# Moving the split of the last row from 640 + 384 to 576 + 448 columns in a row-sum kernel

## The chip, the cores and the metric

The kernel runs on one core of one Trainium2 chip. The metric is the device time of one execution in microseconds (us), the median over several runs. "Span" is the shorter time that the profile covers, from the first to the last instruction of the core. Before the change the first three runs took 162.91 us in the median (162.87 to 163.31).

## The reference

```python
def setup_inputs():
    batch, seq, dim = 32, 512, 1024
    return {"x": np.random.randn(batch, seq, dim).astype(np.float32), "multiplier": 0.5}

def reference(x, multiplier):
    return (np.sum(x, axis=-1) * multiplier).astype(np.float32)
```

There are 16,384 rows of 1024 numbers. Each of the 128 partitions sums 128 of them. 67 MB are read and 64 KB are written.

## The kernel before

The rows of a partition are taken in eight blocks of 16. In seven of them one load brings the whole block; DVE (VectorE) sums rows 0 to 7 and ACT (ScalarE) rows 8 to 15. The last block is loaded in five pieces, so that little is left to do after the last byte. Its last row comes in two parts, and DVE reduces each on its own.

```python
    def dve_span(t, r, lo, hi, dst, start=0.0):
        mid = (lo + hi) // 2
        nc.vector.tensor_tensor_reduce(          # adds the two halves elementwise,
            out=t[:, r, lo:mid],                 # sums the result, begins from `start`
            in0=t[:, r, lo:mid],
            in1=t[:, r, mid:hi],
            scale=mul,
            scalar=start,
            op0=ADD,
            op1=ADD,
            accum_out=dst,
        )

    # ... seven blocks ...

    c0 = (n_blocks - 1) * B
    t = x_pool.tile([P, B, D], fp32, name="xb")
    cut = 640
    pieces = [(0, 8), (8, 13), (13, 15)]
    for lo, hi in pieces:
        loads.append(nc.sync.dma_start(out=t[:, lo:hi, :], in_=x_rows[:, c0 + lo : c0 + hi, :]))
    for lo, hi in ((0, cut), (cut, D)):
        loads.append(nc.sync.dma_start(out=t[:, B - 1, lo:hi], in_=x_rows[:, c0 + B - 1, lo:hi]))
    # ... the store of the first seven blocks ...
    on_act = {4, 5, 6, 7, 11, 12, 14}
    for r in range(B - 1):
        if r in on_act:
            act_row(t, r, c0 + r)
        else:
            dve_span(t, r, 0, D, res[:, c0 + r : c0 + r + 1])
    dve_span(t, B - 1, 0, cut, part)                                      # reduction 1
    dve_span(t, B - 1, cut, D, res[:, rows - 1 : rows], start=part)       # reduction 2
    # ... the store of the last block ...
```

A reduction over N columns is N/2 elementwise sums. It appears in the profile as `CUSTOM_DVE_ANT_0`, followed by a short `DVE_READ_ACCUMULATOR2_ANT` that writes the total. Reduction 2 begins from `part`, the result of reduction 1, so it waits for two things: the landing of part 2, and `part`.

Of the kernel before, what the change touches and what calls it, by code (L numbers as in the profile page):

```python
# [1 line left out]

# [4 lines left out]


@with_exitstack
def kernel(  # L10
    ctx: ExitStack,
    tc: tile.TileContext,
    x: bass.AP,
    multiplier: float,
    out: bass.AP,
):







    nc = tc.nc
    P = nc.NUM_PARTITIONS
    fp32 = mybir.dt.float32
    ADD = mybir.AluOpType.add

    x_flat = x.flatten_outer_dims()
    N, D = x_flat.shape  # L30
    rows = N // P
    x_rows = x_flat.rearrange("(p c) d -> p c d", p=P)
    out_view = out.rearrange("b s -> (b s)").rearrange("(p c) -> p c", p=P)
    mul = float(multiplier)

    B = 16
    n_blocks = rows // B
    assert N == P * rows and rows == n_blocks * B

    x_pool = ctx.enter_context(tc.tile_pool(name="x", bufs=3))  # L40
    res_pool = ctx.enter_context(tc.tile_pool(name="res", bufs=1))
    sums = res_pool.tile([P, rows], fp32, name="sums")
    res = res_pool.tile([P, rows], fp32, name="res")
    part = res_pool.tile([P, 1], fp32, name="part")

    loads = []
    acts = []

    def act_row(t, r, col):
        acts.append(nc.scalar.activation(  # L50
            out=t[:, r, :],
            in_=t[:, r, :],
            func=mybir.ActivationFunctionType.Copy,
            scale=mul,
            accum_out=res[:, col : col + 1],
        ))

    def dve_span(t, r, lo, hi, dst, start=0.0):
        mid = (lo + hi) // 2
        nc.vector.tensor_tensor_reduce(  # L60
            out=t[:, r, lo:mid],
# [9 lines that stand above are left out]
    for b in range(n_blocks - 1):  # L71
        c0 = b * B
        t = x_pool.tile([P, B, D], fp32, name="xb")
        loads.append(nc.sync.dma_start(out=t, in_=x_rows[:, c0 : c0 + B, :]))  # L74
        h = B // 2
        nc.vector.reduce_sum(  # L76
            out=sums[:, c0 : c0 + h], in_=t[:, 0:h, :], axis=mybir.AxisListType.X
        )
        nc.vector.tensor_single_scalar(  # L79
            out=res[:, c0 : c0 + h],  # L80
            in_=sums[:, c0 : c0 + h],
            scalar=mul,
            op=mybir.AluOpType.mult,
        )
        for r in range(h, B):
            act_row(t, r, c0 + r)

    c0 = (n_blocks - 1) * B
    t = x_pool.tile([P, B, D], fp32, name="xb")
    cut = 640  # L90
    pieces = [(0, 8), (8, 13), (13, 15)]
    for lo, hi in pieces:
        loads.append(
            nc.sync.dma_start(  # L94
                out=t[:, lo:hi, :], in_=x_rows[:, c0 + lo : c0 + hi, :]
            )
        )
    for lo, hi in ((0, cut), (cut, D)):
        loads.append(
            nc.sync.dma_start(  # L100
                out=t[:, B - 1, lo:hi], in_=x_rows[:, c0 + B - 1, lo:hi]
            )
        )
    c1 = c0
    nc.sync.dma_start(out=out_view[:, 0:c1], in_=res[:, 0:c1])
# [6 lines that stand above are left out]
    dve_span(t, B - 1, 0, cut, part)  # L112
    dve_span(t, B - 1, cut, D, res[:, rows - 1 : rows], start=part)



    seen = nc.sync.nop()
    for i in loads[-8:] + acts[-1:]:
        tc.add_manual_dep(
            seen.ins,  # L120
            i.ins.name,
            mybir.DependencyInfo(mybir.DependencyClass.Sync, mybir.DependencyReason.DATA),
            reason="ends seen early",
        )
    store = nc.sync.dma_start(out=out_view[:, c1:], in_=res[:, c1:])
    tc.add_manual_dep(
        store.ins,
        seen.ins.name,
        mybir.DependencyInfo(mybir.DependencyClass.NoSync, mybir.DependencyReason.SCHED_ONLY),
        reason="in this order",  # L130
    )

    def start_loads_at_entry(nc_):



        entry, *rest = nc_.main_func.blocks
        is_sp = lambda i: i.engine == mybir.EngineType.SP
        is_load = lambda i: type(i).__name__ == "InstDMACopy"
        for block in rest:  # L140
            body = list(block.instructions)
            own = [i for i in body if is_sp(i)]
            if not any(is_load(i) for i in own):
                continue
            lead = []
            for i in own:
                if not is_load(i) or i.sync_info.on_wait:
                    break
                lead.append(i)
            names = {i.name for i in lead}  # L150
            block.instructions = [i for i in body if i.name not in names]
            head = list(entry.instructions)
            at = next(
                k for k, i in enumerate(head) if is_sp(i) and type(i).__name__ == "InstDrain"
            )
            entry.instructions = head[:at] + lead + head[at:]
            return

    nc.at_finalize(start_loads_at_entry)


# [1 line left out]
_INS = ['x', 'multiplier']  # L163
_OUTS = [((32, 512), 'float32')]

_NUMBERS = {'multiplier': 0.5}


# [26 lines left out]
```

## Time and profile before

| | before |
|---|---|
| median of the first three runs | 162.91 us |
| span of the profiled execution | 160.9 us |
| moved, mean rate | 67.18 MB, 418 GB/s |
| DVE busy, ACT busy | 42%, 42% |
| DMA's share of the chain that ended last | 86% |
| last landing of x to the issue of the last store | 0.715 us |

These lines are from the page of the kernel before: the span, the busy time of the engines, the DMA total, the chain that ended last by engine, and the issues of the last two loads (size, and us from issue to landing).

```profile
span 160.9 us, 236 instructions
...
DVE 68.1 (42%) x34; ACT 67.8 (42%) x127; POOL 0.2 (0%) x4
...
DMA packets 2017, 67.18 MB, mean 418 GB/s; under 512 B 480, under 2 KB 608, under 8 KB 736
...
DMA 86%; DVE 11%; SPq 1%; issue 0%; DVEq 0%
...
xb<-in_x_dram SPq DMA_DIRECT2D x1, 320.0 KB, 47.7
xb<-in_x_dram SPq DMA_DIRECT2D x1, 192.0 KB, 47.6
```

The kernel is bound by its loads. Everything up to the last piece happens while data streams in; only what follows the last bytes can be shortened by the cut. The timeline of the kernel before shows that tail (start in us, duration in us, engine, line, operation, and in brackets the idle time before it with what ended it):

```profile
156.64 0.69 DVE L60 CUSTOM_DVE_ANT_0 xb<-xb 128x512 f32<-128x512 f32 x1 [0.57 <-DMA xb<-in_x_dram]
157.26 0.08 DVE L60 DVE_READ_ACCUMULATOR2_ANT res<- 128x1 f32 x1
157.46 0.49 DVE L60 CUSTOM_DVE_ANT_0 xb<-xb 128x320 f32<-128x320 f32 x1
157.61 0.19 ACT L50 ACTIVATION_READ_ACCUMULATOR xb<-xb 128x1 f32 x1
157.87 0.08 DVE L60 DVE_READ_ACCUMULATOR2_ANT part<- 128x1 f32 x1
158.04 0.42 DVE L60 CUSTOM_DVE_ANT_0 xb<-xb,part 128x192 f32<-128x192 f32 x1
158.38 0.08 DVE L60 DVE_READ_ACCUMULATOR2_ANT res<- 128x1 f32 x1
158.62 0.34 SPq L125 DMA_DIRECT2D out_dram<-res  x1
```

Row 13 is done at 157.34. Reduction 1 is the 128x320 line at 157.46, reduction 2 the 128x192 line at 158.04, and the last store is issued at 158.62. The end of the chain of waits of the same execution (start, duration, what) reads:

```profile
109.78 47.66 DMA xb<-in_x_dram
157.43 0.02 issue
157.46 0.49 DVE xb L60
157.95 0.02 DVE part L60
157.97 0.07 issue
158.04 0.42 DVE xb L60
```

By this chain, part 1's load, then reduction 1, then `part` release reduction 2. "issue" is time in which the engine waited for nothing that the profile shows.

The chain does not show part 2's load. The landing records of the trace do. Each load has 16, one for each DMA engine, and the wait ends with the last of them. To the nanosecond, in us:

```
157.432  last engine of part 1 has landed
157.455  reduction 1 begins
157.873  accumulator read begins; 157.956 it ends, `part` is ready
157.908  last engine of part 2 has landed
157.936  DVE's own wait instruction for part 2 is released (ends 157.957)
158.042  reduction 2 begins
158.623  last store is issued
```

The Trainium skill, "DMA: Bandwidth & Descriptors", section "Why a DMA increments its semaphore by 16 and not by 1", says that each participating engine counts for itself and that only the full 16 mean that all data has landed. The trace agrees: the 16 landings of part 2 spread from 157.143 to 157.908. The separate wait instruction is what "Perfetto Trace Analysis", section "Identifying Dependency Chains", describes: an instruction that waits for several engines may have wait instructions inserted in front of it.

### The profile page before, as it was taken

Reading aid. Unit: us, or ns where it says so; the run is one execution under the profiler, and the core shown is the slowest. Engines: PE = TensorE matmul, PEld = TensorE weight load, DVE = VectorE, ACT = ScalarE, POOL = GpSimd, SP = SyncE. Lnnn points to the kernel's source line nnn. Section 1 sums busy time; section 2 is a strip of 40 time slices with the busy share of each in tenths; the row PEclk is TensorE's granted clock in tenths of the full one; section 3 lists DMA queues with packets and bytes.
Section 4 is the critical chain, followed back from the end, with each engine's and each line's share of the span. In section 5 each row is a group of like instructions: output and inputs, shape, how many; then the busy total and the mean of one; then the engine's idle time right before and its main releaser. Section 6 shows DMA issues by size and latency. Waiting matters only on the chain.

```text
span 160.9 us, 236 instructions
## 1 busy us (share of the span) xinstructions
DVE 68.1 (42%) x34; ACT 67.8 (42%) x127; POOL 0.2 (0%) x4
## 2 busy tenths in 40 slices
DVE  0000049700695008930099102990049700597453
ACT  3000049600694008920099001980039700596952
POOL 0000000000000000000000000000000000000000
DMA  7997997998998998998998998998998998999991
GB/s 261 522 440 342 522 440 342 522 424 359 522 424 359 522 424 359 522 424 359 522 424 361 522 407 375 522 407 375 522 407 375 522 407 375 407 448 396 425 386 40
DMA packets 2017, 67.18 MB, mean 418 GB/s; under 512 B 480, under 2 KB 608, under 8 KB 736
## 3 DMA queue, kind: packets, MB, share of 16 engines
q1 hardware_dynamic: 2016, 67.18, 97.2%
q14 instruction: 1, 0.01, 0.0%
HBM read 67.11 MB, written 0.07 MB: 418 GB/s over the span
## 4 chain that ended last, share of the span: by engine, by line
DMA 86%; DVE 11%; SPq 1%; issue 0%; DVEq 0%
DMA xb<-in_x_dram 86%; DVE sums L76 11%; SPq L94 1%; DVE xb L60 1%; SPq L74 0%; DVE part L60 0%; DVEq L190 0%
## 5 line engine op out<-in xcount | busy, mean ns | idle before, releaser
L50 ACT ACTIVATE xb<-xb 128x1024 f32<-128x1024 f32 x63 | 65.6, 1043 | 88.2 <-DMA xb<-in_x_dram 88.2
L76 DVE TENSOR_REDUCE sums<-xb 128x8 f32<-128x8192 f32 x7 | 60.8, 8686 | 85.0 <-DMA xb<-in_x_dram 85.0
L50 ACT ACTIVATION_READ_ACCUMULATOR xb<-xb 128x1 f32 x63 | 11.8, 187 | 0.0
L60 DVE CUSTOM_DVE_ANT_0 xb<-xb 128x512 f32<-128x512 f32 (+1 forms) x9 | 5.6, 667 | 5.1 <-DMA xb<-in_x_dram 4.9
L50 ACT ACT_TABLE_LOAD x1 | 1.3, 1283 | 1.7 <-PEq L176 1.7
L79 DVE TENSOR_SCALAR res<-sums 128x8 f32<-128x8 f32 x7 | 1.2, 172 | 0.2
L60 DVE DVE_READ_ACCUMULATOR2_ANT res<- 128x1 f32 x9 | 0.7, 83 | 0.0
L60 DVE CUSTOM_DVE_ANT_0 xb<-xb,part 128x192 f32<-128x192 f32 x1 | 0.4, 419 | 0.1
L176 POOL MEMSET const-uint8-127<- 128x1 uint8 x1 | 0.1, 103 | 0.0
L176 POOL MEMSET const-bfloat16-1.0<- 128x1 bf16 x1 | 0.1, 102 | 0.0
L176 POOL MEMSET const-float32-0.0<- 128x1 f32 x1 | 0.1, 99 | 0.2 <-issue 0.2
L176 POOL MEMSET const-float32-1.0<- 128x1 f32 x1 | 0.1, 99 | 0.0
L60 DVE DVE_READ_ACCUMULATOR2_ANT part<- 128x1 f32 x1 | 0.1, 83 | 0.0
## 6 DMA issues: line engine op xcount, KB each, us to landing
xb<-in_x_dram SPq DMA_DIRECT2D x1, 4096.0 KB, 39.6
xb<-in_x_dram SPq DMA_DIRECT2D x1, 2560.0 KB, 45.4
xb<-in_x_dram SPq DMA_DIRECT2D x1, 1024.0 KB, 47.4
xb<-in_x_dram SPq DMA_DIRECT2D x1, 320.0 KB, 47.7
xb<-in_x_dram SPq DMA_DIRECT2D x1, 192.0 KB, 47.6
xb<-in_x_dram SPq DMA_DIRECT2D x7, 49.3
out_dram<-res SPq DMA_DIRECT2D x1, 56.0 KB, 10.8
out_dram<-res SPq DMA_DIRECT2D x1, 8.0 KB, 1.4
```

The lines of the kernel that those rows point to most:

```text
L50: acts.append(nc.scalar.activation(out=t[:, r, :], in_=t[:, r, :], func=mybir.ActivationFunctionType.Copy, scale=mul, accum_out=res[:, col ...
L60: nc.vector.tensor_tensor_reduce(out=t[:, r, lo:mid], in0=t[:, r, lo:mid], in1=t[:, r, mid:hi], scale=mul, scalar=start, op0=ADD, op1=ADD, ...
L76: nc.vector.reduce_sum(out=sums[:, c0 : c0 + h], in_=t[:, 0:h, :], axis=mybir.AxisListType.X)
L79: nc.vector.tensor_single_scalar(out=res[:, c0 : c0 + h], in_=sums[:, c0 : c0 + h], scalar=mul, op=mybir.AluOpType.mult,)
L94: nc.sync.dma_start(out=t[:, lo:hi, :], in_=x_rows[:, c0 + lo : c0 + hi, :])
L176: nc = _bacc.Bacc("TRN2", target_bir_lowering=False, num_devices=1)
```

## The change

The cut between the two parts moves 64 columns to the left. Part 1 gets smaller, so it should land and be reduced sooner, while reduction 2 grows by 32 sums.

```diff
-    cut = 640
+    cut = 576
```

## The prediction

> **What bounds the kernel now.** DMA. The page gives 67.18 MB at a mean 418 GB/s over a span of 160.9 us; DVE and ACT are each busy 42%. The chain of waits is 86% DMA `xb<-in_x_dram`; it ends with the landing of the last row's first part, two DVE reductions of that row and the last store. Only this tail can change: bytes and instruction count stay.
>
> **The tail before** (timeline and landing records of the trace, us from the span's start):
> - Part 1 (640 columns): all sixteen engines landed at 157.432. DVE was free at 157.34 and waited for it; reduction 1 (320 sums, 493 ns) began at 157.455.
> - Its accumulator read, which makes `part`, ran 157.873 to 157.956.
> - Part 2 (384 columns) landed at 157.908. DVE waits for it in an instruction of its own, released at 157.936, 28 ns after the landing, ended at 157.957.
> - Reduction 2 (192 sums, starts from `part`, 419 ns) began at 158.042. Its accumulator read ended at 158.468, the store was issued at 158.623 and landed at 160.04.
>
> So reduction 2 had two releasers that tie within a nanosecond: `part` (157.956) and the wait for part 2 (157.957). The landing of this block's rows 0 to 7 shows the same form of wait binding: landed 148.035, released 148.063, again 28 ns.
>
> **What the change does.**
> 1. Part 1 shrinks from 2560 to 2304 B a partition. Packets took 103 ns (2560 B) and 66 ns (1536 B): 37 ns per 1024 B, so 94 and 75 ns after. Each engine moves eight of each: part 1 lands 8 x 9.4 = 75 ns sooner, at about 157.36. The sum per engine is unchanged, so part 2 still lands at about 157.91.
> 2. Reduction 1: 288 sums. The Trainium skill, "VectorE: DVE Perf Modes", section "The TRN2 errata", gives (N+151)/0.96 ns for an fp32 tensor_tensor. The trace agrees: 691 ns for 512 (687 to 693 measured), 491 for 320 (493). So 33 ns less; begin 157.38, `part` ready at about 157.85, 0.11 us sooner than now.
> 3. Reduction 2: 224 sums, 33 ns more, about 452 ns.
>
> **What lies on the critical path.** The 0.11 us that `part` gains is not collected: reduction 2 is then held by part 2's landing alone, which stays. It begins where it did (158.04 to 158.05) and takes 33 ns longer. The end and the store move 0.03 to 0.04 us later. The tie says 640 was already the balance point; 576 gives DVE more work after the last byte. Had part 2's landing not bound, the gain would have been 0.11 - 0.03 = 0.08 us, so even the rival is 0.05%.
>
> Predicted: 162.95 us (162.91 + 0.03 to 0.04), range 162.60 to 163.40. The range comes from the runs of before (162.87 to 163.31), far wider than the effect. Chances: faster by over 2% 0.01, within 2% 0.98, slower by over 2% 0.01.
>
> **What in the profile would show each step.**
> - The gap between the landings of parts 1 and 2 grows from 0.476 to about 0.55 us.
> - Reduction 1 about 460 ns, reduction 2 about 452 ns.
> - Reduction 2 begins about 0.135 us after part 2's landing (as now), but 0.19 us after `part` was ready (now 0.086).
> - The chain that ended last passes through part 2's DMA, not part 1 and reduction 1.
> - Last landing of x to the store's issue: 0.715 us before, about 0.75 after.
>
> **What would make it wrong.** Part 2 lands sooner because its packets or its completion cost less than the straight line says; then up to 0.08 us is gained. Or 1792 and 2304 B rows move worse than 1536 and 2560 B; then tenths are lost. Ordinary run-to-run noise would hide all of it.

## The result, and the profile after

| | before | after |
|---|---|---|
| median of 6 runs | 163.01 us | 163.11 us |
| lowest to highest | 162.87 to 163.31 | 162.90 to 163.16 |
| ratio, 95% interval | | 1.0003, 0.999 to 1.0016 |
| span of the profiled execution | 160.9 us | 161.3 us |

A ratio here is the mean time of one kernel's fast runs over that of the other's fast runs of the same rounds, so it is not quite the ratio of the medians in the table. The time is the same within 2%, and indeed within 0.2%.

The lines of the page of the kernel after that answer to those of before:

```profile
span 161.3 us, 236 instructions
...
DVE 68.1 (42%) x34; ACT 67.9 (42%) x127; POOL 0.2 (0%) x4
...
DMA packets 2017, 67.18 MB, mean 417 GB/s; under 512 B 480, under 2 KB 608, under 8 KB 736
...
DMA 86%; DVE 11%; SPq 1%; issue 0%; DVEq 0%
...
xb<-in_x_dram SPq DMA_DIRECT2D x1, 288.0 KB, 47.6
xb<-in_x_dram SPq DMA_DIRECT2D x1, 224.0 KB, 47.6
```

The bound is the same, and so are the bytes and the number of instructions. The timeline of the kernel after, same columns as before:

```profile
157.07 0.69 DVE L60 CUSTOM_DVE_ANT_0 xb<-xb 128x512 f32<-128x512 f32 x1 [0.57 <-DMA xb<-in_x_dram]
157.69 0.08 DVE L60 DVE_READ_ACCUMULATOR2_ANT res<- 128x1 f32 x1
157.79 0.46 DVE L60 CUSTOM_DVE_ANT_0 xb<-xb 128x288 f32<-128x288 f32 x1
158.03 0.19 ACT L50 ACTIVATION_READ_ACCUMULATOR xb<-xb 128x1 f32 x1
158.18 0.08 DVE L60 DVE_READ_ACCUMULATOR2_ANT part<- 128x1 f32 x1
158.46 0.45 DVE L60 CUSTOM_DVE_ANT_0 xb<-xb,part 128x224 f32<-128x224 f32 x1 [0.20 <-DMA xb<-in_x_dram]
158.83 0.08 DVE L60 DVE_READ_ACCUMULATOR2_ANT res<- 128x1 f32 x1
159.07 0.34 SPq L125 DMA_DIRECT2D out_dram<-res  x1
```

Two things are new. Reduction 1 is shorter (0.46) and reduction 2 longer (0.45). And DVE now stands idle 0.20 us in front of reduction 2, waiting for the DMA; the line of before had no such bracket. The end of the chain of waits of the kernel after:

```profile
110.70 47.62 DMA xb<-in_x_dram
158.32 0.03 issue
158.35 0.02 DVEq L60
158.37 0.09 issue
158.46 0.45 DVE xb L60
```

The chain now goes from part 2's load straight to DVE's wait instruction (`DVEq`) and reduction 2. `part` has left it.

The whole tail lies about 0.42 us later in this profile than in the one of before. That is not the cut: the load of rows 13 and 14, which comes ahead of anything the change touches, already landed 0.43 us later (157.049 against 156.621). Counted from that landing, part 1 landed after 0.720 us, against 0.811 before, and part 2 after 1.275 us, against 1.287 before. The experiments below show how much the arrival of the stream scatters.

### The profile page after: what moved, and what is told of

Read it like the earlier page. It is cut to its first block, busy times and chain, and to the rows that moved or that the text cites. A ratio compares the mean times of both kernels' runs of the same rounds, so it can differ in the third digit from the quotient of the medians.

```text
span 161.3 us, 236 instructions
## 1 busy us (share of the span) xinstructions
DVE 68.1 (42%) x34; ACT 67.9 (42%) x127; POOL 0.2 (0%) x4
## 4 chain that ended last, share of the span: by engine, by line
DMA 86%; DVE 11%; SPq 1%; issue 0%; DVEq 0%
DMA xb<-in_x_dram 86%; DVE sums L76 11%; SPq L94 1%; SPq L100 0%; DVE xb L60 0%; SPq L74 0%; DVEq L60 0%; DVEq L190 0%
## 5 line engine op out<-in xcount | busy, mean ns | idle before, releaser
L60 DVE CUSTOM_DVE_ANT_0 xb<-xb,part 128x224 f32<-128x224 f32 x1 | 0.5, 452 | 0.2 <-DMA xb<-in_x_dram 0.2
```

The lines of the kernel that those rows point to most:

```text
L60: nc.vector.tensor_tensor_reduce(out=t[:, r, lo:mid], in0=t[:, r, lo:mid], in1=t[:, r, mid:hi], scale=mul, scalar=start, op0=ADD, op1=ADD, ...
```

## The experiments

The theory is the prediction's: after the change reduction 2 is held by the landing of part 2, which doesn't move, and the only lasting effect is the 33 ns that reduction 2 grew by. Rival 1: the new row sizes (2304 and 1792 bytes) slow the loads, and this is where the first profile's extra 0.45 us of span come from. Rival 2: `part` still holds reduction 2, so that an earlier part 1 is worth something. Rival 3, for cuts to the right of 640: the landing of part 2 alone sets the end.

The measure is the *tail*, from the last landing of part 2 to the issue of the last store. It is the sum of three terms: landing to the beginning of reduction 2, the duration of reduction 2, and a rest of 0.160 to 0.164 us in every run. All are read from the records of each profile. All profiles had a granted clock of 1.0. Each row is one profile. The terms repeat well from profile to profile: where the landing holds reduction 2 behind the usual wait instruction, it begins after 132 to 135 ns; reduction 2 of one size and form differs by 2 ns at most; and the rest differs by 4 ns. The effect of 34 ns is well above that.

The tail starts at part 2's landing, so it cannot show whether that landing itself moved. Counted from the landing of rows 13 and 14, part 2 landed after 1.263 to 1.289 us in the five profiles with loads of 576 and 448 columns, and after 1.274 to 1.290 us in the three with 640 and 384. So no shift shows, but one as small as the effect would be lost in this scatter.

| run | gap, landing of part 1 to part 2 | `part` ready, after part 2's landing | reduction 2 begins, after part 2's landing | reduction 2 takes | tail |
|---|---|---|---|---|---|
| before (640) | 0.476 us | +0.048 us | 0.134 us | 419 ns | 0.715 us |
| after (576) | 0.555 | -0.064 | 0.134 | 452 | 0.749 |
| after_again (576) | 0.549 | -0.058 | 0.133 | 451 | 0.748 |
| compute_only | 0.471 | +0.019 | 0.134 | 452 | 0.748 |
| load_only | 0.537 | -0.046 | 0.133 | 417 | 0.712 |
| cut128 | 1.066 | -0.383 | 0.134 | 684 | 0.979 |
| cut668b | 0.441 | +0.098 | 0.135 | 404 | 0.700 |
| cut768 | 0.323 | +0.267 | 0.302 | 352 | 0.817 |
| cut896 | 0.165 | +0.490 | 0.526 | 285 | 0.974 |
| cut768_nopart | 0.293 | not waited for | 0.214 | 284 | 0.661 |
| part_in_row (640) | 0.468 | +0.055 | 0.132 | 361 | 0.655 |
| in_row668 | 0.480 | +0.057 | 0.133 | 347 | 0.640 |
| part_first576b | 0.559 | -0.068 | 0.164 | 451 | 0.777 |
| part_first_in_row576b | 0.529 | -0.037 | 0.163 | 395 | 0.721 |

### The changed kernel again

No edit; five timed rounds.

> The changed kernel once more, timed in five rounds. Theory (reduction 2 is held by the landing of part 2; only its own 33 ns are added): last landing of x to the store's issue 0.75 us again (0.749 in the first profile of after, 0.715 before), ratio 1.0002, which no timing here can tell from 1. Rival 1 (the 0.45 us by which the first profile of after is longer comes from the new row sizes, which slow the stream): ratio about 1.0025 and the first block again landing some 0.36 us later than in before. I expect the theory; the stream's arrival should scatter by tenths of a microsecond in both kernels.

Measured: tail 0.748 us. 162.94 us against 162.88 for before, ratio 1.0003 (0.9991 to 1.0016). The load of rows 13 and 14 landed at 156.768 us here, against 157.049 us in the first profile of the same kernel. In all profiles it landed between 156.62 and 157.15, although the code up to there is the same. So the extra span of the first profile is scatter of the stream, and rival 1 has no support: its ratio of 1.0025 lies outside the interval.

### The same move, eight times as far

```diff
-    cut = 640
+    cut = 128
```

> The same move, eight times as far: cut 128, part 2 of 896 columns (448 sums). Theory: reduction 2 begins 0.134 us after part 2's landing as before, takes 419 + 256 x 1.04 = 686 ns, so last landing to the store's issue is 0.715 + 0.267 = 0.98 us, and the time grows by 0.27 us, ratio about 1.0016. The gap between the landings of parts 1 and 2 is 896 x 1.235 ns = 1.11 us. Rival 2 (`part` still holds reduction 2): `part` is ready more than half a microsecond before the landing, so reduction 2 would begin before or at the landing and the tail would not grow by the whole 0.27 us. Rival 1: the stream itself lands later by more than the scatter.

Measured: `part` is ready 0.383 us before part 2 lands, and reduction 2 begins 0.134 us after the landing, just as before. It takes 684 ns. Tail 0.979 us, 0.264 more than before. 163.09 us against 162.88, ratio 1.0017 (1.0003 to 1.0031). This is the one place where a timing sees the effect, and at the expected size. Rival 2 falls for cuts to the left of 640.

The gap came out at 1.07 us instead of 1.11, a small miss.

### The compute half alone

Loads of 640 and 384 columns, reductions of 576 and 448.

```diff
-    dve_span(t, B - 1, 0, cut, part)
-    dve_span(t, B - 1, cut, D, res[:, rows - 1 : rows], start=part)
+    dve_span(t, B - 1, 0, 576, part)
+    dve_span(t, B - 1, 576, D, res[:, rows - 1 : rows], start=part)
```

> The compute half of the change alone: loads stay 640 and 384 columns, the reductions are 576 and 448 columns. Theory: the gap between the landings stays 0.476 us, reduction 2 (452 ns) begins 0.134 us after part 2's landing, last landing to the store's issue 0.749 us: all of the loss with no change of a transfer. Rival 1 (the row sizes of the loads matter): 0.715 us as before.

Measured: gap 0.471 us, reduction 2 begins after 0.134 us and takes 452 ns, tail 0.748 us. All of the loss is there without any change of a transfer.

### The load half alone

Loads of 576 and 448 columns, but reduction 2 leaves 64 columns out (a wrong result, relative error 0.02).

```diff
-    cut = 640
+    cut = 576
@@
-    dve_span(t, B - 1, cut, D, res[:, rows - 1 : rows], start=part)
+    dve_span(t, B - 1, 640, D, res[:, rows - 1 : rows], start=part)
```

> The load half of the change alone, WRONG RESULT ON PURPOSE in the last column of the output: loads are 576 and 448 columns, reduction 1 takes 576 columns, reduction 2 only the last 384 (64 columns are left out). Theory: gap between landings 0.55 us, `part` ready 0.2 us before reduction 2 begins, which is still 0.134 us after part 2's landing; reduction 2 419 ns; last landing to the store's issue back at 0.715 us: the 0.11 us that `part` gains buys nothing. Rival 2 (`part` holds reduction 2 and the loads' shift would be worth it): 0.64 us or less.

Measured: `part` is ready 0.046 us before part 2's landing, 0.094 us sooner against it than in before, and reduction 2 begins 0.133 us after the landing all the same. Tail 0.712 us, as before within 3 ns. The timeline of this run shows where the gain of `part` goes, into the bracket of the last line:

```profile
157.71 0.46 DVE L60 CUSTOM_DVE_ANT_0 xb<-xb 128x288 f32<-128x288 f32 x1
...
158.09 0.08 DVE L60 DVE_READ_ACCUMULATOR2_ANT part<- 128x1 f32 x1
158.35 0.42 DVE L60 CUSTOM_DVE_ANT_0 xb<-xb,part 128x192 f32<-128x192 f32 x1 [0.18 <-DMA xb<-in_x_dram]
```

So inside the tail the transfers' half is worth nothing, and the arithmetic half costs 33 ns. Together they are the change.

### The cut moved the other way

```diff
-    cut = 640
+    cut = 896
```

> The cut moved the other way: 896 and 128 columns. Theory (640 is the balance point): now `part` holds reduction 2. Gap between landings 128 x 1.235 = 0.16 us; reduction 1 (448 sums, about 626 ns) makes `part` ready about 0.66 us after part 1's landing; reduction 2 (64 sums, about 286 ns) begins about 0.086 us later, 0.585 us after part 2's landing; last landing to the store's issue 0.585 + 0.209 + 0.239 = 1.03 us, 0.32 us more than before; ratio about 1.002. Rival (the landing of part 2 alone sets the end whatever the cut): less work after the last byte, 0.582 us, ratio below 1.

Measured: reduction 2 begins 0.526 us after the landing, tail 0.974 us; 163.11 against 162.92 us, ratio 1.0008 (0.9995 to 1.0022), which does not exclude 1. Rival 3 expected 0.582 us and falls: `part` holds reduction 2 here. But the theory's own number, 1.03 us, was 0.06 us too high. Of this, 0.05 us are one step: it had taken 86 ns from `part` to reduction 2, read from before, and the run shows 36 ns.

```diff
-    cut = 640
+    cut = 768
```

> 768 and 256 columns. Theory: gap 0.316 us, reduction 2 (128 sums, 352 ns) begins 0.086 us after `part`, about 0.36 us after part 2's landing; last landing to the store's issue 0.87 us. Rival (landing alone): 0.65 us.

Measured: tail 0.817 us, again 0.05 us under the expectation, again because reduction 2 begins 35 ns after `part`. The end of its chain of waits shows it:

```profile
158.19 0.10 DVE part L60
158.28 0.02 issue
158.31 0.35 DVE xb L60
```

Here 0.02 us of "issue" follow `part`, where before had 0.07. A release by `part` took 35 and 36 ns in these two runs. So the 86 ns in before were no release by `part`: the chain named it because it was the later of the two events that it could see, but what reduction 2 really waited for was the wait instruction for part 2, which sits in front of it and takes its time after the landing.

### The wait for `part` taken away at 768 columns

Reduction 2 begins from zero, so it needs no `part` (a wrong result, relative error 0.08).

```diff
-    cut = 640
+    cut = 768
@@
-    dve_span(t, B - 1, cut, D, res[:, rows - 1 : rows], start=part)
+    dve_span(t, B - 1, cut, D, res[:, rows - 1 : rows])
```

> 768 and 256 columns, reduction 2 starts from 0 and not from `part`, WRONG RESULT ON PURPOSE in the last column. It takes the wait for `part` away by taking its data away. Theory: reduction 2 begins as soon as reduction 1 lets the engine go, about 0.2 us after part 2's landing instead of 0.36; without the scalar operand it takes 290 ns ((128+151)/0.96) instead of 352; last landing to the store's issue about 0.65 us. If `part` was not what held reduction 2 at 768 columns, it begins at 0.36 us as in the run with it.

Measured: reduction 2 begins 0.214 us after the landing instead of 0.302, at the very nanosecond at which reduction 1's accumulator read begins, so it waits only for its engine. It takes 284 ns instead of 352. Tail 0.661 us. At 768 columns `part` was what held it.

### Where the balance really lies

```diff
-    cut = 640
+    cut = 668
```

> 668 and 356 columns. In the runs where `part` was clearly last (768 and 896 columns) reduction 2 began 36 ns after `part` was ready, not 86; where the landing was clearly last it began 134 ns after the landing. If both hold, before had no tie: `part` would have allowed 157.992 and the landing 158.042, 50 ns of slack at 640. The two cross where 50 ns is used up at 1.235 + 0.521 ns per column: 28 columns further, at 668. Expected: `part` ready 0.099 us after part 2's landing, reduction 2 begins 0.135 us after it, last landing to the store's issue 0.701 us, 14 ns less than at 640. If my reading of a tie at 640 was right, reduction 2 begins 0.086 us after `part`, 0.185 us after the landing, and the tail is 0.75 us.

Measured: `part` is ready 0.098 us after the landing, reduction 2 begins after 0.135 us, tail 0.700 us. The reading of a tie at 640 expected 0.75 and falls. It begins 37 ns after `part`, so both releasers are at their limit here: they cross at about 668, and this cut saves 0.015 us over 640. (The run's one time, 163.16 us, says little: its rows 13 and 14 landed at 157.144 us, late in the scatter of the stream.)

### Shortening what comes after the landing

The reduction with the scalar operand `part` took 60 to 62 ns more than the prediction's formula for its size, (N+151)/0.96 ns for N sums, in every run (419 against 357 ns before). In this version reduction 1 writes its unscaled total into the row itself, in front of part 2, and reduction 2 reads it there as one of its columns.

```diff
-    dve_span(t, B - 1, 0, cut, part)
-    dve_span(t, B - 1, cut, D, res[:, rows - 1 : rows], start=part)
+    dve_span(t, B - 1, 0, cut - 2, t[:, B - 1, cut - 2 : cut - 1], scale=1.0)
+    dve_span(t, B - 1, cut - 2, D, res[:, rows - 1 : rows])
```

(`dve_span` gets an argument `scale=mul`, which it passes on.)

This kernel is not right, although the texts call it so. Reduction 1 takes columns 0 to 637 and writes its total over column 638, so that column of x is never summed. Worked out from the reference's inputs, this is a relative error of 0.0025 of the whole output (0.0027 for the cut of 668), where leaving out 64 columns made 0.021. The same holds for the other two kernels that keep the partial sum in the row. What they show of the cost of the operand stands; a right kernel of this form was not run.

> A version meant to beat both: cut 640 as before, but the partial sum is written (unscaled) into column 638 of the row, and reduction 2 reads it there as data (386 columns, 193 sums) and starts from 0. Right result. Expected: the 62 ns by which the reduction with the scalar operand exceeds (N+151)/0.96 (419 against 357 ns for 192 sums) go away: reduction 2 takes 358 ns, it begins 0.134 us after part 2's landing (tie with the partial sum as before), last landing to the store's issue 0.655 us, 0.06 us less than before. Ratio 0.9996, not to be told from 1 by timing. If the 62 ns belong to something else, reduction 2 takes 420 ns.

Measured: reduction 2 takes 361 ns for 193 sums, tail 0.655 us; 162.90 against 162.92 us, ratio 0.9995 (0.9983 to 1.0008). Some 60 ns went away with the scalar operand, the waits being the same, so they belong to it. Together with the cut of 668:

> The partial sum in the row (which took the tail to 0.655 us at 640 columns) at the measured balance point of 668 columns. Right result. Expected: reduction 2 (179 sums, about 347 ns) begins 0.135 us after part 2's landing, last landing to the store's issue 0.64 us, 0.075 us less than before, the shortest tail of all kernels run; ratio 0.9995, not to be told from 1 by timing.

Measured: tail 0.640 us, the shortest of all, 0.075 us less than before; 162.90 against 162.96 us, ratio 0.9995 (0.998 to 1.0011). By the trace its tail is shorter than that of both kernels, but it leaves a column out, so the gain is not shown for a right result; by its time it cannot be told from the kernel before.

### An attempt that showed nothing

Reduction 1 begins 22 to 25 ns after its landing when DVE is free, reduction 2 needs 134 ns after its own. If the difference comes from the separate wait instruction in front of reduction 2, letting DVE wait for `part` first and for the landing last should save 0.1 us.

```diff
     dve_span(t, B - 1, 0, cut, part)
+    ready = nc.vector.nop()
+    # ... `ready` waits for reduction 1, reduction 2 is ordered after `ready` ...
     dve_span(t, B - 1, cut, D, res[:, rows - 1 : rows], start=part)
```

> Loads and reductions as in the changed kernel (576 and 448), but DVE waits for `part` in an instruction of its own in front, so that reduction 2 itself carries only the wait for part 2's landing, as reduction 1 does for part 1's. Reduction 1 begins 22 to 24 ns after its landing in all runs but one (where DVE was not free), reduction 2 134 ns. Expected, if it is the separate wait in front of it that makes the difference: reduction 2 begins 0.02 to 0.03 us after part 2's landing, last landing to the store's issue 0.64 us instead of 0.749. If the 134 ns belong to the second reduction whatever waits where, 0.75 us. If the order of the waits turns out as in the changed kernel, nothing is shown.

The second kernel also keeps the partial sum in the row:

> The last two ideas together at 576 columns, right result: `part` goes into the row and is waited for first, reduction 2 (225 sums, about 393 ns) carries the wait for the landing alone. Expected: reduction 2 begins 0.025 us after part 2's landing (or about 0.04 us if `part` is just late), last landing to the store's issue 0.58 us, 0.135 us less than before; ratio 0.9992, which five rounds may not tell from 1.

Measured: the two waits were merged into one instruction that still waited for the landing in front of reduction 2, and took 50 ns instead of 21. Reduction 2 began after 0.164 and 0.163 us, the tails were 0.777 and 0.721 us; the second kernel took 162.91 against 162.90 us, ratio 1.0003 (0.9987 to 1.0018). The order of the waits was not changed, so these runs show only that 29 ns more in the wait instruction begin it 29 to 30 ns later.

The traces at hand say more. The first row of the last block is also reduced behind a wait instruction of its own (for rows 0 to 7), with no `part` and no scalar operand, and DVE stands idle before it (0.8 us in before). In the 14 profiles it begins 138 to 145 ns after that landing (144 ns in before), while every DVE reduction that carries the wait for its load itself, and finds DVE free, begins after 22 to 25 ns. So in these traces the long delay goes with the separate wait instruction and not with reduction 2 alone. What happens in the 84 to 96 ns between the end of that instruction and the reduction, no run shows.

## Why the prediction was right, and where it was not

- **Time.** Predicted 162.95 us; measured 163.11, with before at 163.01 in the same six runs. Both are within the range, and the interval of the ratio covers the predicted 1.0002. That is no evidence for the mechanism: the range is 0.8 us wide, and the rival's gain of 0.08 us would have lain in it as well. The times cannot confirm a shift of 0.03 us; the trace does.
- **Part 1 lands sooner, part 2 where it did.** Predicted gap 0.55 us; measured 0.555 and 0.549. Counted from the landing of rows 13 and 14, part 1 came after 0.720 and 0.740 us instead of 0.811, and part 2 after 1.275 and 1.289 us against 1.287. The straight line through the packet times (103 and 66 ns) gave 94 and 75 ns for the new sizes; the new packets took 94 and 76 on average. Right, as far as the scatter of 0.03 us in part 2's landing lets one see.
- **The reductions.** Predicted 460 and 452 ns, measured 459 and 452. The Trainium skill's (N+151)/0.96 ns ("VectorE: DVE Perf Modes", "The TRN2 errata") held within 8 ns for every reduction without a scalar operand, from 64 sums (221 ns, formula 224) to 512 (683 to 693 ns, formula 691). (The 512-sum reductions of before took 685 to 693 ns, not 687 to 693 as the prediction has it.)
- **The gain of `part` is not collected.** Right: `part` was ready 0.064 us before the landing, and reduction 2 began 0.134 us after the landing, unchanged. The load half alone gained nothing (0.712 us) and the compute half alone lost it all (0.748 us).
- **The end moves 0.03 to 0.04 us.** Right: the tail went from 0.715 to 0.749 us.
- **"So reduction 2 had two releasers that tie within a nanosecond", and "640 was already the balance point".** Wrong. The prediction compared the end of `part` with the end of the wait instruction, as if reduction 2 took 86 ns from either. It takes 35 to 37 ns from `part` (768, 896 and 668 columns) and 134 from the landing. In before, `part` would have allowed a start at about 157.992 and the landing allowed 158.042: the landing held it alone, with about 50 ns to spare, and the balance lies near 668. The prediction had the counterexample in hand: it cites the wait for rows 0 to 7, released 28 ns after its landing, but not that the reduction behind it began 144 ns after the landing with no `part` to wait for. The error did no harm to the forecast, and that is luck: the change moved away from the balance, to the side where the landing holds in any case. For a cut to the right it would have mattered, and there two of the expectations missed by 0.05 and 0.06 us.

## What to carry to other kernels

When two inputs release one instruction, making one of them earlier buys nothing once the other holds it; ask what each alone would allow, with its own latency from event to start, and find the crossing. A chain of waits names the later event, not the one with the longer way to the engine: an "issue" gap after the named releaser (0.07 us) that is longer than the same gap where that releaser surely binds (0.02 us) said here that something else held it. And moving work from before the last byte to after it cost its full duration here, for 32 sums (33 ns) as for 256 (265 ns), while a load-bound stream whose arrival scatters by 0.5 us hides it from the timing.

## What the Trainium skill lacked or had wrong

- "VectorE: DVE Perf Modes", "The TRN2 errata": the formula for tensor_tensor held within 8 ns (measured 221 to 693 ns). The page does not give what a per-partition scalar operand adds. Here a reduction that starts from a [128, 1] operand took 60 to 62 ns more than the formula at 64, 128, 178, 192, 224 and 448 sums, and the extra went away when the same value was read as data.
- "Perfetto Trace Analysis", "Identifying Dependency Chains": it says that waits may be put into instructions of their own. It does not say what the two forms cost. Here a load that the reduction itself waits for was followed by it after 22 to 25 ns, one that a separate wait instruction stood for after 132 to 135 ns (reduction 2) and 138 to 145 ns (the first row of the last block), and a result of the same engine after 35 to 37 ns. Why the second form takes so much longer, no run settled.
- "DMA: Bandwidth & Descriptors" gives no measure of how much the arrival of a long stream varies from run to run. Here the same load of the same stream landed between 156.62 and 157.15 us after the start of the span, in 14 profiles.
